# Adding up squares with accumulating transfers instead of VectorE, in a Strassen-like matmul with GELU

## The chip, the cores and the metric

The kernel runs on one core of a Trainium2 chip. Its time is the device time of one execution in microseconds; three executions gave 1578.17, 1579.82 and 1580.01 us, so the median before the change is 1579.82 us. The profile is of one more execution, with a span of 1577.1 us from the first to the last instruction and a granted TensorE clock of 0.999.

The engines are named as in the profile: PE is TensorE (PEld its weight loads), DVE is VectorE, ACT is ScalarE, POOL is GpSimd, and SP is SyncE. GpSimd issues all loads of this kernel, SyncE all stores.

## The reference

```python
def setup_inputs():
    m, k, n = 4096, 4096, 4096
    return {
        "a": np.random.randn(m, k).astype(np.float32),
        "b": np.random.randn(k, n).astype(np.float32),
    }

def reference(a, b):
    x = np.matmul(a, b)
    return 0.5 * x * (1 + np.tanh(np.sqrt(2 / np.pi) * (x + 0.044715 * x**3)))
```

The output is float32, 4096 x 4096.

## The kernel before

A and B are cast to float16 on their way in and cut into quadrants. Four quadrants of a block of the output (two times 512 rows by two times 512 columns) are made from seven products of sums of quadrants instead of eight plain products. That is one group; there are 16, numbered gi = 0 to 15. A group has 7 products s of 4 steps q each, 28 steps, and each step is 16 matmuls of 128x128 by 128x512. (Half of the first group is computed plainly, while its data come in: 16 plain steps and 14 others.) The products are accumulated in two chains of PSUM banks, X and Y, and between two products ScalarE or VectorE takes a copy of the banks:

```python
PRODUCTS = [
    ("M3", "Y", "11", ("12", "22", 1)),
    ("M5", "X", ("11", "12", -1), "22"),
    ("M7", "X", ("12", "22", -1), ("21", "22", 1)),
    ("M1", "X", ("11", "22", -1), ("11", "22", -1)),
    ("M4", "X", "22", ("21", "11", 1)),
    ("M2", "Y", ("22", "21", -1), "11"),
    ("M6", "Y", ("21", "11", -1), ("11", "12", 1)),
]
# ... cut
def multiply(gi, s, q):
    name, chain = product(gi, s)[:2]
    first = q == 0 and name in ("M3", "M5")
    sa, sb = sums.pop((gi, s, q))
    for i in range(RT):                       # RT = 4 banks
        acc = bank(gi, chain, i) if first else banks[chain, i]
        products(acc, sa, sb, i, first, q == QPH - 1)   # 4 matmuls, L331
        if q == QPH - 1:
            settle(gi, name, i)               # copies by ACT, sums by DVE, y
```

Such a copy is, for M5, `m5 = keep("m5", X, 2)`, a copy on ScalarE from PSUM (L395), after which VectorE makes `y = Y - m5`. M7, M1 and M4 go on in the same X banks.

VectorE makes the sums of quadrants that a step needs (L302), two steps ahead (AHEAD = 2), from A tiles (aT) and B tiles (bR) into aS and bS. The order of the program is the order on each engine; every engine works through its own queue in order:

```python
for n, step in enumerate(steps):
    for fn, args in before.get(n, ()):        # loads, transposes, squares, checks
        fn(*args)
    if n + AHEAD < len(steps):
        gi, s, q = steps[n + AHEAD]
        if s >= 0:
            make_sums(gi, s, q)
    if step[:2] != (0, 2):
        flush()
    combine()
    if step[1] < 0:
        plain(n)
    else:
        multiply(*step)
    if step == (0, 2, QPH - 1):
        flush()
```

Loads of the next group's B tiles stand in GpSimd's queue at steps 13, 15, 17 and 19 (8 transfers of 128 KB each) and at steps 25 and 27 (16 each).

The kernel also checks its inputs: it adds up the squares of all elements of A and B, by rows and columns, and takes another path (cut here) if they spread too far for float16. Half of the groups do this work: b in groups 1, 5, 9, 13 and a in groups 2, 6, 10, 14. A group has 32 pieces of 128x1024 elements, two a step for the first six steps and then one a step:

```python
def square(which, blk, quad, c, h):
    # ... src: a piece of an aT or bR tile
    half = quad[which == "b"]
    if half not in energy:
        t = energy[half] = pool.tile([P, W], BF16, name="energy", tag=f"energy{half}")
    else:
        t = pool.tile([P, W], BF16, name="square", tag="square", bufs=2)
        squares.append((half, t))
    nc.scalar.activation(t[:, :], src, ACT.Square)             # L207

def add_squares():
    for half, t in squares:
        tt(energy[half], energy[half], t, ALU.add)             # L431, on DVE
    squares.clear()

def weigh(which):          # DVE: an addition, a transpose and a reduction for each half
    ...

for mb in range(NMB):
    for which, gi in (("b", mb * NNB + 1), ("a", mb * NNB + 2)):
        # ... pieces: quadrants "22", "12", "21", "11"; c in 0, 1; h in 0..3
        n_two = len(pieces) - NP * QPH + 2
        for x, piece in enumerate(pieces):
            n = max(x // 2, x - n_two)
            at(gi, n // QPH, n % QPH, square, which, blk, *piece)
            at(gi, (n + 1) // QPH, (n + 1) % QPH, add_squares)
        at(gi, 6, 2, weigh, which)
```

So a group has two first squares, which go straight to `energy`, and 30 that go through the two buffers named `square` and are added.

Before the first data are there, TensorE multiplies zeros to keep its clock up:

```python
N_WARM = 46
def warm():
    z = pool.tile([P, NC], F16, name="zeros", tag="bS", bufs=AHEAD + 1)
    nc.vector.memset(z[:, :], 0.0)
    # ... banks
    for _ in range(N_WARM):
        nc.tensor.matmul(banks["X", RT - 1][:, :], z[:, :P], z[:, :], start=True, stop=True,
                         skip_group_check=True)                # L343
```

Of the kernel before, what the change touches and what calls it, by code (L numbers as in the profile page):

```python
# [13 lines left out]
ALU = mybir.AluOpType  # L14
# [10 lines left out]
AHEAD = 2  # L25
# [15 lines left out]
NP = len(PRODUCTS)  # L41
QPH = 4
# [6 lines left out]
    ("22", "21", "12", True), ("22", "22", "22", True),  # L49
]  # L50
N_PLAIN = 2 * len(PLAIN)
N_WARM = 46


SQUARE_MAX = 2.0**26
# [45 lines left out]
def half_path(  # L101
# [9 lines left out]
    nc = tc.nc  # L111
# [76 lines left out]
    def part(tiles, blk, quad, q):  # L188

        t = tiles[blk, quad, q // 2].rearrange("p x y -> p (x y)")  # L190
        w = 4 * NC
        return t[:, (q % 2) * w : (q % 2 + 1) * w]

    energy, squares = {}, []
# [13 lines left out]

    def add_squares():
        for half, t in squares:  # L210
            tt(energy[half], energy[half], t, ALU.add)
        squares.clear()

    def weigh(which):
# [63 lines left out]
    def product(gi, s):  # L278
        return (LAST if gi == len(groups) - 1 else PRODUCTS)[s]

    def make_sums(gi, s, q, only=None, h=None):

        mb, nb = groups[gi]
        _, _, oa, ob = product(gi, s)
        got = []
        for tiles, blk, o, tag in ((a_tiles, mb, oa, "aS"), (b_tiles, nb, ob, "bS")):
            if only not in (None, tag):
                continue
            if isinstance(o, str):
                got.append(part(tiles, blk, o, q))  # L290
                continue
            t = sums.pop((tag, gi, s, q), None)
            if t is None or h:
                if t is None:
                    t = pool.tile([P, 4 * NC], F16, name=tag, tag=tag, bufs=AHEAD + 1)
                x, y, z = t[:, :], part(tiles, blk, o[0], q), part(tiles, blk, o[1], q)
                if h is not None:
                    x, y, z = (
                        v.rearrange("p (jj m) -> p jj m", jj=2)[:, :, h * TM : (h + 1) * TM]
                        for v in (x, y, z)  # L300
                    )
                nc.vector.tensor_tensor(  # L302
                    out=x, in0=y, in1=z, op=ALU.add if o[2] > 0 else ALU.subtract
                )
            got.append(t)
            if tag == only:
                sums[tag, gi, s, q] = t
                return
        sums[gi, s, q] = got
# [10 lines left out]
    def bank(gi, chain, i):  # L320
        par = (gi + (chain == "Y")) % 2
        t = psum_pool.tile([P, NC], F32, name=f"acc{chain}", tag=f"bank{par}{i}")
        banks[chain, i] = t
        return t
# [11 lines left out]
# [3 lines that stand above are left out]
        for i in range(RT):  # L339
            bank(0, "X", i)  # L340
            bank(0, "Y", i)
        for _ in range(N_WARM):
            nc.tensor.matmul(  # L343
                banks["X", RT - 1][:, :], z[:, :P], z[:, :], start=True, stop=True, skip_group_check=True
            )

    def plain(n):

        (quad, oa, ob, by_rows), h = PLAIN[n // 2], n % 2
        chain = "X" if quad == "11" else "Y"  # L350
        seen = [x for x in range(len(PLAIN)) if PLAIN[x][0] == quad]
        sa, sb = a_tiles[0, oa, 0], b_tiles[0, ob, 0]
        sa = sa.rearrange("p jj (m e) -> p jj m e", e=2)
        tiles = [(j, e) for j in range(NJ // 2) for e in range(2) if by_rows or e == h]
        for i in range(h * RT // 2, (h + 1) * RT // 2) if by_rows else range(RT):
            acc = banks[chain, i]
            kept = quad in ("11", "22")
            start = (n // 2 == seen[0] or not kept) and (by_rows or h == 0)
            stop = (n // 2 == seen[-1] or not kept) and (by_rows or h == 1)
            c = f"c{quad}"  # L360
            for j, e in tiles:
                nc.tensor.matmul(
                    acc[:, :], sa[:, j, i * P : (i + 1) * P, e], sb[:, 2 * j + e, :],
                    start=start and (j, e) == tiles[0], stop=stop and (j, e) == tiles[-1],
                    skip_group_check=True,
                )
            if not stop:
                continue
            if not kept and n // 2 == seen[1]:
                tt(post[c, i], post[c, i], acc, ALU.add)  # L370
            elif quad == "12":
                post[c, i] = keep("x1", acc, RT)
            elif quad == "11":
                tt(post["c12", i], post["c12", i], acc, ALU.add)
            elif quad == "21":
                tag = ("energy1", "energy2", "square", "square")[i]
                t = pool.tile([P, W], BF16, name="c21", tag=tag, bufs=1 + (i > 1)).bitcast(F32)
                nc.scalar.copy(out=t[:, :], in_=acc[:, :])
                post[c, i] = t
            else:  # L380
                tt(post["c12", i], post["c12", i], acc, ALU.subtract)
# [5 lines that stand above are left out]
        for i in range(RT):  # L387
            acc = bank(gi, chain, i) if first else banks[chain, i]
            products(acc, sa, sb, i, first, q == QPH - 1)
            if q == QPH - 1:  # L390
                settle(gi, name, i)
# [8 lines left out]
    def flush():  # L400

        for args in waiting:
            gi, i, ih, jh, y, _ = args
            plain_part = post.pop((f"c{ih + 1}{jh + 1}", i), None) if gi == 0 else None
            if plain_part is not None:
                tt(y, y, plain_part, ALU.add)
            emit(*args)
        waiting.clear()
# [3 lines left out]
    def combine():  # L412

        for gi, i in later:
            x7, x1 = post["x7", i], post["x1", i]
            tt(x7, x1, x7, ALU.subtract)
            tt(x1, banks["Y", i], x1, ALU.subtract)
        later.clear()

    def emit(gi, i, ih, jh, y, src):  # L420
        mb, nb = groups[gi]
        nc.scalar.activation(y[:, :], src[:, :], ACT.Gelu_apprx_tanh)  # L422
        r0 = ih * MH + mb * TM + i * P
        c0 = jh * NH + nb * NC
        nc.sync.dma_start(out=out[r0 : r0 + P, c0 : c0 + NC], in_=y[:, :])
# [4 lines left out]
    def tt(o, x, y, op):  # L430
        nc.vector.tensor_tensor(out=o[:, :], in0=x[:, :], in1=y[:, :], op=op)  # L431
# [40 lines left out]
    steps = [(0, -1, n) for n in range(N_PLAIN)]  # L472
# [5 lines left out]
    def at(gi, s, q, fn, *args):  # L478
        if gi == 0 and s >= 0:
            q = max(q, QPH // 2)  # L480
        before.setdefault(position[gi, s, q], []).append((fn, args))


    for n, whats in (
# [10 lines left out]
        for what in whats.split():  # L495
            half = what[-1] == "0" and what != "A11_0" or what in ("A22_1", "T22_1")
# [52 lines left out]
    for mb in range(NMB):  # L549
        for which, gi in (("b", mb * NNB + 1), ("a", mb * NNB + 2)):  # L550
# [6 lines left out]
            for x, piece in enumerate(pieces):  # L557
                n = max(x // 2, x - n_two)
# [18 lines left out]
    at(len(groups) - 1, 2, 2, answer)  # L577
    at(len(groups) - 1, 4, 0, read)

    with tc.manual_schedule():  # L580
        warm()
        table = pool.tile([P, 1], F32, name="table", tag="table")
        nc.vector.memset(table[:, :], 0.0)
        nc.scalar.activation(table[:, :], table[:, :], ACT.Gelu_apprx_tanh)
        for n, step in enumerate(steps):
            for fn, args in before.get(n, ()):
                fn(*args)
            if n + AHEAD < len(steps):
                gi, s, q = steps[n + AHEAD]
                if s >= 0:  # L590
                    make_sums(gi, s, q)
            if step[:2] != (0, 2):
                flush()
            combine()
# [3 lines that stand above are left out]
                multiply(*step)  # L598
            if step == (0, 2, QPH - 1):
                flush()  # L600
        flush()
    return said["value"]


def kernel(tc: tile.TileContext, a: bass.AP, b: bass.AP, out: bass.AP):
    stands = half_path(tc, a, b, out)
    with tc.If(stands == 0):
        general_path(tc, a, b, out)
# [30 lines left out]
```

## Time and profile before

| what | value |
|---|---|
| time, median of 3 | 1579.82 us |
| span of the profile | 1577.1 us |
| TensorE busy | 1567.7 us, 7246 products |
| VectorE busy | 1233.7 us |
| ScalarE busy | 518.0 us |
| GpSimd busy (issuing transfers) | 537.7 us |
| DMA packets | 225047, 211.13 MB |
| HBM | 285.22 MB read, 67.11 MB written |

In a line of the groups stand the source line, the engine, the operation, what is written and read with its shape, how often, then the busy time in us and the mean of one in ns, and after the second bar the idle time of the engine just before these instructions and what ended most of it. A line of the waits names who waited for whom, the total in us, how often, and the longest. A line of the timeline begins with the start and the duration in us, and ends, in brackets, with the engine's idle time ahead of it and what ended that. For a transfer, the duration on POOL is the time to issue it; the time to landing is counted from the start of that issue to the semaphore that tells of its last byte.

### The profile page before, as it was taken

How to read it: one execution, taken by the hardware profiler on the slowest of the kernel's cores; microseconds unless marked ns; L12 is line 12 of the kernel's file. 1: busy time of each engine (PE TensorE's matmuls, PEld its weight loads, DVE VectorE, ACT ScalarE, POOL GpSimd, SP SyncE). 2: the span in 40 equal slices, each digit the busy share in tenths (PEclk: the TensorE clock that was granted, in tenths of full speed). 3: DMA queues.
4: the chain of work that ended last, by engine and by line, in shares of the span. 5: the costliest groups of instructions: out<-in, count | busy, mean ns of one | idle time of the engine just before them, and what ended most of it. 6: DMA issues, size and time to landing. Idle time of an engine off the chain costs nothing. (4 is left out here: it accounts for less than half of the span.)

```text
span 1577.1 us, 19678 instructions
## 1 busy us (share of the span) xinstructions
PE 1567.7 (99%) x7246; PEld 709.6 (45%) x7246; DVE 1233.7 (78%) x1381; ACT 518.0 (33%) x710; POOL 537.7 (34%) x980
## 2 busy tenths in 40 slices
PE   9999999999999999999999999999999999999998
PEld 4444444444444444444444444444444444444443
DVE  1698888967787888895778778887687778988775
ACT  1036445311122545531111344542211145364111
POOL 7753442420234144341124413245011443314400
PEclk9999999999999999999999999999999999999999
DMA  9999884882968378686597937679468885747802
GB/s 173 198 215 189 132 162 79 161 162 48 193 106 158 87 131 160 108 179 115 87 161 117 186 72 142 146 113 182 79 121 146 134 160 93 151 105 134 161 28 82
DMA packets 225047, 211.13 MB, mean 134 GB/s; under 512 B 20144, under 2 KB 192176, under 8 KB 224944
## 3 DMA queue, kind: packets, MB, share of 16 engines
q0 software_dynamic: 187648, 142.67, 61.7%
q1 hardware_dynamic: 37296, 67.13, 11.8%
q8 instruction: 59, 0.97, 0.2%
q14 instruction: 44, 0.36, 0.1%
HBM read 285.22 MB, written 67.11 MB: 223 GB/s over the span
## 5 line engine op out<-in xcount | busy, mean ns | idle before, releaser
L331 PEld LDWEIGHTS <-aS 128*128 128x128 f16 x4960 | 485.3, 98 | 587.2 <-issue 2.2
L186 POOL DMA_DIRECT2D bR<-in_b_dram x832 | 447.6, 544 | 700.0 <-DVE bS L302 329.7
L302 DVE TENSOR_TENSOR aS<-aT 128x2048 f16<-128x2048 f16 (+1 forms) x312 | 376.1, 1212 | 151.0 <-PE accX L331 114.5
L331 PE MATMUL accX<-bS,aS 128*128 128x512 f16 x1984 | 431.1, 379 | 0.0
L302 DVE TENSOR_TENSOR bS<-bR 128x2048 f16<-128x2048 f16 x310 | 376.1, 1218 | 69.3 <-PE accX L331 58.5
L331 PEld LDWEIGHTS <-aT 128*128 128x128 f16 x1984 | 194.2, 98 | 234.8 <-issue 0.8
L422 ACT ACTIVATE y<-y 128x512 f32<-128x512 f32 x192 | 118.5, 630 | 351.8 <-DVE y L431 351.4
L331 PE MATMUL accY<-bS,aS 128*128 128x512 f16 x992 | 216.7, 379 | 1.8 <-DVE y L431 1.8
L331 PE MATMUL accY<-bS,aT 128*128 128x512 f16 x992 | 216.9, 379 | 0.5 <-DVE bS L302 0.5
L331 PE MATMUL accX<-bS,aT 128*128 128x512 f16 x992 | 216.7, 379 | 0.0
L331 PE MATMUL accX<-bR,aS 128*128 128x512 f16 x992 | 216.7, 379 | 0.0
L331 PE MATMUL accY<-bR,aS 128*128 128x512 f16 x992 | 216.7, 379 | 0.0
L186 POOL DMA_DIRECT2D stage<-in_a_dram x144 | 89.9, 630 | 249.0 <-DVE aT L161 178.0
L431 DVE TENSOR_TENSOR energy<-energy,square 128x1024 bf16<-128x1024 bf16 x240 | 164.4, 685 | 9.5 <-ACT square L207 5.7
L395 ACT COPY x<-accX 128x512 f32<-128x512 f32 x128 | 74.9, 585 | 224.3 <-PE accX L331 224.3
L207 ACT ACTIVATE square<-aT 128x1024 bf16<-128x1024 f16 x120 | 123.4, 1051 | 70.6 <-DVE energy L431 70.2
L207 ACT ACTIVATE square<-bR 128x1024 bf16<-128x1024 f16 x120 | 123.0, 1050 | 62.5 <-DVE energy L431 60.5
L161 DVE STREAM_TRANSPOSE aT<-stage 128x2048 uint32<-128x2048 uint32 (+1 forms) x37 | 74.6, 2017 | 46.0 <-DMA stage<-in_a_dram 39.9
L395 ACT COPY m<-accX 128x512 f32<-128x512 f32 x60 | 34.7, 579 | 215.7 <-PE accX L331 213.6
L422 ACT ACTIVATE y<-accX 128x512 f32<-128x512 f32 x64 | 38.2, 597 | 100.1 <-PE accX L331 99.9
L431 DVE TENSOR_TENSOR x<-accX,x 128x512 f32<-128x512 f32 x64 | 44.0, 691 | 21.8 <-ACT y L422 19.1
L431 DVE TENSOR_TENSOR y<-accY,m 128x512 f32<-128x512 f32 x60 | 39.9, 687 | 12.5 <-ACT m L395 12.4
(38 smaller groups left out, 344.9 us busy)
## 6 DMA issues: line engine op xcount, KB each, us to landing
bR<-in_b_dram POOLq DMA_DIRECT2D x832, 128.0 KB, 5.2
out_dram<-y SPq DMA_DIRECT2D x256, 256.0 KB, 5.7
stage<-in_a_dram POOLq DMA_DIRECT2D x112, 256.0 KB, 6.8
stage<-in_a_dram POOLq DMA_DIRECT2D x32, 128.0 KB, 5.1
row<-seen_d SPq DMA_DIRECT2D x2, 1.5 KB, 4.2
seen_d<-seen SPq DMA_DIRECT2D x1, 3.0 KB, 7.4
```

The source lines that it names most:

```text
L161: nc.vector.transpose(dst[:, :, x, :], src[:, :, x, :])
L186: nc.gpsimd.dma_start(out=dst, in_=src)
L207: nc.scalar.activation(t[:, :], src, ACT.Square)
L302: nc.vector.tensor_tensor(out=x, in0=y, in1=z, op=ALU.add if o[2] > 0 else ALU.subtract)
L331: nc.tensor.matmul(acc[:, :], sa[:, j // 2, i * P : (i + 1) * P, j % 2], sb[:, j, :], start=start and j == 0, stop=stop and j == 3, skip_g ...
L395: nc.scalar.copy(out=t[:, :], in_=src[:, :])
L422: nc.scalar.activation(y[:, :], src[:, :], ACT.Gelu_apprx_tanh)
L431: nc.vector.tensor_tensor(out=o[:, :], in0=x[:, :], in1=y[:, :], op=op)
```

## The change

Three things change. The squares are no longer added by VectorE (`tt`) but by transfers from GpSimd's queue that add what they read to what stands at their destination, both in on-chip memory: 128 partitions x 1024 bf16 elements, 256 KB, 30 for each of the eight groups. This is to take 240 instructions off VectorE. Second, in the first group the sums for M6's last step are made after the step that ends M2, so that VectorE comes to M2's y first and TensorE gets M6's banks earlier. (The sums concerned are named `late`.) Third, there are 39 warm products instead of 46.

```diff
-N_WARM = 46
+N_WARM = 39
...
     def add_squares():
         for half, t in squares:
-            tt(energy[half], energy[half], t, ALU.add)
+            nc.gpsimd.dma_start(out=energy[half][:, :], in_=t[:, :], accum_op=ALU.add)
         squares.clear()
...
+    late = (0, NP - 1, QPH - 1)
+
     with tc.manual_schedule():
...
             if n + AHEAD < len(steps):
-                gi, s, q = steps[n + AHEAD]
-                if s >= 0:
-                    make_sums(gi, s, q)
+                ahead = steps[n + AHEAD]
+                if ahead[1] >= 0 and ahead != late:
+                    make_sums(*ahead)
             if step[:2] != (0, 2):
                 flush()
...
             if step == (0, 2, QPH - 1):
                 flush()
+            if step == (0, NP - 2, QPH - 1):
+                make_sums(*late)
         flush()
```

In the order of the changed kernel's instructions each of these transfers waits for the one before it into the same half, for ScalarE's square, and for the transfer that last used its semaphore; a square waits for the transfer that read its buffer two squares ago. In GpSimd's queue a group's 30 additions stand as 16, a burst of 8 loads, 2, 8 loads, 2, 8 loads, 2, 8 loads, 6, 16 loads, 2, 16 loads.

## The prediction

> **What bounds the kernel now.** I read the page first (shares of the engines, then the groups), then who waited for whom, then the timeline of the first 45 us and of the stretch from 215 to 315 us, which is one of the groups that the squares belong to, and last the time to landing of each kind of transfer. The chain of waits on the page holds a single link (ACT, 0%) and says nothing here.
>
> ```profile
> PE 1567.7 (99%) x7246; PEld 709.6 (45%) x7246; DVE 1233.7 (78%) x1381; ACT 518.0 (33%) x710; POOL 537.7 (34%) x980
> ```
>
> TensorE is busy 99% of the span. The timeline shows 32 products starting at 14.37 and the next 32 at 21.27, so one step of 16 products takes 3.45 us. 7246 less 46 warm ones are 7200 products, 450 steps, 1553 us. Together with the 14.4 us ahead of them and about 6 us behind the last product's start this is 1573 of 1577.1 us: TensorE waits for about 4 us in all. No part of the change can win more than that, since it removes no product that counts.
>
> ```profile
> L431 DVE TENSOR_TENSOR energy<-energy,square 128x1024 bf16<-128x1024 bf16 x240 | 164.4, 685 | 9.5 <-ACT square L207 5.7
> L207 ACT ACTIVATE square<-aT 128x1024 bf16<-128x1024 f16 x120 | 123.4, 1051 | 70.6 <-DVE energy L431 70.2
> L207 ACT ACTIVATE square<-bR 128x1024 bf16<-128x1024 f16 x120 | 123.0, 1050 | 62.5 <-DVE energy L431 60.5
> ```
>
> These groups are what the change touches: 240 additions of 685 ns on VectorE. The reader is to see the last column: ScalarE's squares already wait 130.7 us for VectorE's additions to free one of the two square buffers. That idle time costs nothing today, but it is the hook on which a slower adder pulls. Who pulls next is seen in the waits:
>
> ```profile
> ACT m L395 <- PE accX L331: 213.6, 30, 45.8
> ACT square L207 <- DVE energy L431: 130.7, 96, 4.7
> ...
> PE accY L331 <- DVE y L431: 1.8, 1, 1.8
> ```
>
> The last line is one of the few waits of TensorE: 1.8 us, once. In the timeline it stands at 113.72, the start of M6 in the first group: VectorE makes M6's last operand sums (110.72 and 111.85) ahead of y (112.99), and M6 needs the bank that y empties.
>
> ```profile
> 220.45 1.04 ACT L207 ACTIVATE energy<-aT 128x1024 bf16<-128x1024 f16 x1
> ...
> 237.34 2.00 ACT L207 ACTIVATE square<-aT 128x1024 bf16<-128x1024 f16 x2 [3.75 <-DVE energy L431]
> 243.25 0.58 ACT L395 COPY m<-accX 128x512 f32<-128x512 f32 x1 [3.90 <-PE accX L331]
> ```
>
> ```profile
> 141.05 1.76 POOL L186 DMA_DIRECT2D bR<-in_b_dram  x3 [0.20 <-issue]
> 163.05 4.27 POOL L186 DMA_DIRECT2D bR<-in_b_dram  x8 [20.25 <-DVE energy L431]
> ```
>
> ```profile
> 229.17 0.54 POOL L186 DMA_DIRECT2D bR<-in_b_dram  x1 [0.80 <-DMA bR<-in_b_dram]
> 260.25 4.28 POOL L186 DMA_DIRECT2D bR<-in_b_dram  x8 [30.54 <-DVE bS L302]
> ```
>
> The first of these is ScalarE in group 2, which starts at 218.0: fourteen squares stand in its in-order queue ahead of the m copies, which empty M5's banks. Today they are through by 239.3 and ScalarE then waits 3.9 us for TensorE. The two others are GpSimd's queue: the loads that stand in front of the squares' additions are issued until 142 us in group 1 (start 120.6) and until 229.7 in group 2.
>
> ```profile
> L186 POOL DMA_DIRECT2D bR<-in_b_dram x832: 542/542/579, 4.2 to 1486.5; - x167
> ...
> DMA to landing us min/median/max: 2.8/5.2/9.7
> ```
>
> ```profile
> q0 software_dynamic: 187648, 142.67, 61.7%
> q1 hardware_dynamic: 37296, 67.13, 11.8%
> ```
>
> A 128 KB load issued by GpSimd takes 2.8 us at the least from issue to landing. The two queues give the time of a packet: 0.617 x 16 x 1577.1 / 187648 = 83 ns on q0, 0.118 x 16 x 1577.1 / 37296 = 80 ns for the 2 KB rows of the stores on q1.
>
> **What the Trainium skill says.** "DMA: Bandwidth & Descriptors", Anatomy of one DMA (SWDGE path), gives some 2.0 us fixed for such a transfer, mostly completion, plus its bytes. The trace agrees: 2.8 us less 128 packets / 16 engines x 83 ns = 0.66 leaves 2.1. The same page, Rules for kernel authors, says that nothing holds the bytes between an accumulate's read and its write, and that the next must wait for the earlier one's semaphore; in the order of the changed kernel every addition waits for the one before it. "Collectives: The Full Stack", the bandwidth ceiling in Part 3, says that an add in the DMA engine costs two source reads and so runs at half the rate of a copy; no run here shows that yet. "TensorE: Matmul & The Clock Gate", Part 1, says that after an idle window of about 3.4 us the array restarts at half clock; here the first warm products start 0.43 us apart and later ones 0.216, so it can be seen at the start at least.
>
> **The change part by part.**
> 1. 39 warm products. The 46 end at about 14.1 us (the first 13 at 0.43 us, the other 33 at 0.2157: 1.42 + 5.6 + 7.1), and the transpose that releases the first real product ends at 11.75 + 2.37 = 14.12. Both end together, so seven fewer give at best 0.2 us; the 1.5 us of idle time that they leave is short of an idle window. I count 0.
> 2. The sums moved behind y. y can follow the sums at 109.58, and M6 starts where M2 ends. The moved sums then end near the start of M6's last step and may give 0.4 us back. I count 1.5 us won.
> 3. VectorE loses 240 x 0.685 = 164 us. TensorE hardly waits for it (one 0.5 us wait for bS in group 1), so I count 0.5 us.
> 4. The squares, in 8 of the 16 groups (1, 2, 5, 6, 9, 10, 13, 14), 30 additions each. They become one serial chain on GpSimd's queue: each needs the landing of the one before. Its period p is the 2.8 us, less 0.66, plus an estimate of 128 x 2 KB rows read twice, 8 x 2 x 80 ns = 1.28, which gives 3.4; with 0.2 us to pick up the semaphore (the gap between POOL issues in the timeline) p = 3.6 us. The chain then stops TensorE in three places of a group.
>
> **M5's copies.** In a b group (1, 5, 9, 13) thirteen buffered squares stand ahead of the copies, with two buffers, so the copies need the 11th addition, one more square (1.05) and a copy (0.6). In an a group a second first square needs no buffer, and it is the 10th. Group 1: the last load ahead is issued at 142.3, the first addition lands behind the queued loads at about 148.6, ten more make 184.6, the copy is done at 186.3; M7 needs the bank at 120.6 + 8 x 3.45 = 148.2. Stall 38 us. Groups 5, 9, 13: the loads ahead end 10.7 us after the group's start, not 22, so 27 us. The a groups follow a stalled group, their loads ahead end some 8.5 us after the start, and they need nine more: 21 us. 38 + 3 x 27 + 4 x 21 = 203.
>
> **M1's and M4's copies** (steps 15 and 19). Between them stand four additions, 14.4 us, against four steps, 13.8, and a burst of 8 loads of B for each two additions. A burst takes 8 x 0.66 = 5.3 us of the DMA engines, of which I add 4 us to the chain. By step 15 the chain is 1 us late in a b group and 4.5 in an a group; by step 19 two bursts add 14.4 + 8 - 13.8 = 8.6. About 10 and 13 us: 4 x 10 + 4 x 13 = 92.
>
> **The weighing at step 26.** VectorE must wait for the last addition, and the next group's first sum is behind it. Eight additions, a burst of 8 and one of 16 (10 us): 28.8 + 14 = 42.8, less the 1.7 by which the copies trail; then weighing 4.15 us (308.77 to 312.92 in the timeline of VectorE) and a sum of 1.2, against 8 steps, 27.6. Stall 19, and 8 x 19 = 152.
>
> Sum: 1579.8 - 2 + 203 + 92 + 152 = 2025. A transfer that reads SBUF should land somewhat earlier than the HBM load that I took p from, so I choose 2000.
>
> **The rivals.**
> (a) The chain is hidden: additions land fast enough for ScalarE and the loads. For it: VectorE's slack grows and POOL is busy for only 34%. Against it: 11 additions in the 16 us that group 2 leaves between 229.7 and 245.6 need 1.4 us each, half of the fastest landing in the profile. Time 1577.
> (b) Only throughput counts: 240 x 128 packets x 160 ns / 16 = 307 us more on engines that are some 74% busy. In the groups of the squares (70 to 82% busy in the view by stretches) 38 us are added to 97, about 10 to 20 us over: 1580 + 8 x 15 = 1700.
> (c) The adder in the DMA engine is slow, far below half rate: p of 6 us instead of 3.6 adds 30 x 2.4 x 8 = 576 us: about 2600.
> (d) The clock: each stall over a window restarts TensorE with 13 products at half clock, 2.8 us. Up to 24 stalls make 67 us, but what follows is bound by the chain again, so most of it vanishes in the next stall. I add nothing.
>
> **Range and chances.** The time moves by 240 us for each microsecond of p, since the chain has 240 links. p from 2.6 to 4.9 gives about 1760 to 2320, and I hold that at 8 in 10. Faster by over 2% would be more than the 4 us there are: 0.01. Within 2% needs rival (a): 0.05. Slower: 0.94.
>
> **What would show it.** Right: GpSimd's additions follow each other at 3 to 4.5 us; ScalarE's squares wait for those transfers; TensorE waits for ScalarE (copies of m) at the start of M7 in eight groups, 20 to 40 us each, and for VectorE's sums at the start of the next group behind a wait of the weighing; groups 0, 3, 4, 7, 8, 11, 12, 15 keep their 96.7 us; no wait of M6 in the first group. Wrong: landings of 2 us or less with TensorE still at 99%; DMA engines near full with additions landing late because of bytes, not of their order; or long waits of TensorE for B tiles, which I do not expect, because the loads of the next group stand 15 steps ahead of their use.

## The result and the profile after

The changed kernel takes 2127.28 us (median, 2120.36 to 2133.84) against 1579.28 for the kernel before: the ratio is 1.347, 95% interval 1.344 to 1.350. The profiled execution spans 2118.8 us, 541.7 more than before, with a mean granted TensorE clock of 0.888.

The shares of the engines, from the page of the changed kernel:

```profile
PE 1626.0 (77%) x7239; PEld 721.2 (34%) x7239; DVE 1086.6 (51%) x1141; ACT 516.4 (24%) x710; POOL 753.2 (36%) x1220
```

VectorE is relieved as intended, by 147 us. TensorE now stands idle for 23% of a longer span, and no engine is near full: this is a kernel bound by latency. The groups that tell so:

```profile
L331 PE MATMUL accX<-bS,aS 128*128 128x512 f16 x1984 | 445.8, 387 | 194.9 <-ACT m L395 193.6
...
L211 POOL DMA_DIRECT2D energy<-square x240 | 211.6, 882 | 728.6 <-DMA energy<-square 383.4
...
L331 PE MATMUL accY<-bS,aT 128*128 128x512 f16 x992 | 233.2, 399 | 208.1 <-DVE bS L302 208.1
...
L207 ACT ACTIVATE square<-bR 128x1024 bf16<-128x1024 f16 x120 | 126.3, 1055 | 389.0 <-DMA energy<-square 388.9
```

After the second bar the first of these two groups of matmuls, which stood idle for 0.0 and 0.5 us in the kernel before, waits 194.9 us, 193.6 of them for ScalarE's copies of M5, and the second 208.1 us for VectorE's first sum of a group. ScalarE's squares wait for the transfers, and GpSimd, which issues the transfers, waits for the transfers. The same ring in the waits:

```profile
ACT square L207 <- DMA energy<-square: 732.0, 204, 19.6
...
PE accY L331 <- DVE bS L302: 208.1, 9, 27.8
DVE square L220 <- DMA energy<-square: 199.6, 7, 30.3
PE accX L331 <- ACT m L395: 193.6, 9, 38.1
...
PE accY L331 <- DVE aS L302: 54.1, 8, 9.3
```

The counts are the reader's clue: eight groups add squares, and TensorE's long waits come in eights and nines, not spread over the 112 products. How long a landing takes, from the view of the transfers' destination:

```profile
L211 POOL DMA_DIRECT2D energy<-square x240: 860/869/998, 143.9 to 2004.8; - x120
...
DMA to landing us min/median/max: 3.2/3.3/9.0
```

Now the ring link by link, in group 1. GpSimd's timeline, then ScalarE's, then TensorE's:

```profile
180.28 0.87 POOL L211 DMA_DIRECT2D energy<-square  x1 [2.95 <-DMA energy<-square]
184.07 0.87 POOL L211 DMA_DIRECT2D energy<-square  x1 [2.92 <-DMA energy<-square]
187.88 0.87 POOL L211 DMA_DIRECT2D energy<-square  x1 [2.94 <-DMA energy<-square]
```

```profile
183.62 1.06 ACT L207 ACTIVATE square<-bR 128x1024 bf16<-128x1024 f16 x1 [2.73 <-DMA energy<-square]
187.43 1.06 ACT L207 ACTIVATE square<-bR 128x1024 bf16<-128x1024 f16 x1 [2.76 <-DMA energy<-square]
188.40 1.05 ACT L395 COPY m<-accX 128x512 f32<-128x512 f32 x2
```

```profile
136.91 13.98 PE L331 MATMUL accX<-bR,aS 128*128 128x512 f16 x64
189.02 26.34 PE L331 MATMUL accX<-bS,aS 128*128 128x512 f16 x112 [38.13 <-ACT m L395]
```

The addition issued at 184.07 is the group's eleventh. It lands at 187.4, the thirteenth square starts at 187.43, the copy of M5's first bank ends at 189.0, and M7 starts at 189.02, 38.1 us late. The end of the group, GpSimd's timeline first, then VectorE's and TensorE's:

```profile
271.35 0.87 POOL L211 DMA_DIRECT2D energy<-square  x1 [2.96 <-issue]
271.91 4.67 POOL L186 DMA_DIRECT2D bR<-in_b_dram  x8
...
284.27 0.96 POOL L211 DMA_DIRECT2D energy<-square  x1
290.11 0.87 POOL L211 DMA_DIRECT2D energy<-square  x1 [4.89 <-issue]
```

```profile
293.69 0.42 DVE L220 TENSOR_TENSOR square<-energy 128x512 bf16<-128x512 bf16 x1 [28.57 <-DMA energy<-square]
...
297.30 2.35 DVE L302 TENSOR_TENSOR bS<-bR 128x2048 f16<-128x2048 f16 x2
```

```profile
298.57 15.82 PE L331 MATMUL accY<-bS,aT 128*128 128x512 f16 x64 [25.50 <-DVE bS L302]
```

VectorE stands for 28.6 us in front of the weighing, with the next group's sums behind it in its queue. By stretches, groups 1 to 4 (the columns are span, then busy time and instructions of PE, PEld, DVE, ACT, POOL, then granted clock, DMA share, GB/s):

```profile
118.80:298.60 179.80, 103.46 (x450) 45.16 (x449) 65.56 (x72) 48.67 (x62) 74.41 (x119) 0.80 0.76 136
298.60:455.20 156.60, 105.97 (x449) 45.81 (x449) 65.82 (x71) 47.55 (x60) 61.39 (x95) 0.83 0.73 132
455.20:553.90 98.70, 98.70 (x448) 44.26 (x448) 72.70 (x71) 16.81 (x29) 17.01 (x27) 0.98 0.61 109
553.90:650.60 96.70, 96.70 (x449) 43.84 (x448) 71.57 (x70) 17.11 (x30) 32.52 (x60) 1.00 0.79 137
```

Groups 1 and 2 lose 83 and 60 us against the 96.7 us of before. Group 3 takes 98.7 us, its first products at a lower rate after the stop ahead of it, and group 4 takes 96.7. The DMA engines are busy for 0.76 and 0.73 of the time in groups 1 and 2 and for 0.79 in group 4, which loses nothing.

Summed over the starts of all products of the trace, the loss splits into idle time of TensorE at step 8 of the groups (194 us), at steps 16 and 22 (28 and 55), at step 0 of the next group (207), and some 55 us in which it ran at less than full rate after such a stop: 539 of the 541.7 us.

### The profile page after: what moved, and what is told of

Its sections match the earlier page's. It is cut to its first block, busy times and chain, and to the rows that moved or that the text cites. A ratio compares the mean times of both kernels' runs of the same rounds, so it can differ in the third digit from the quotient of the medians.

```text
span 2118.8 us, 19959 instructions
## 1 busy us (share of the span) xinstructions
PE 1626.0 (77%) x7239; PEld 721.2 (34%) x7239; DVE 1086.6 (51%) x1141; ACT 516.4 (24%) x710; POOL 753.2 (36%) x1220
## 5 line engine op out<-in xcount | busy, mean ns | idle before, releaser
L331 PEld LDWEIGHTS <-aS 128*128 128x128 f16 x4960 | 492.2, 99 | 861.6 <-issue 238.9
L331 PE MATMUL accX<-bS,aS 128*128 128x512 f16 x1984 | 445.8, 387 | 194.9 <-ACT m L395 193.6
L186 POOL DMA_DIRECT2D bR<-in_b_dram x832 | 464.5, 675 | 254.4 <-PE accX L331 87.3
L211 POOL DMA_DIRECT2D energy<-square x240 | 211.6, 882 | 728.6 <-DMA energy<-square 383.4
L331 PE MATMUL accY<-bS,aT 128*128 128x512 f16 x992 | 233.2, 399 | 208.1 <-DVE bS L302 208.1
L331 PEld LDWEIGHTS <-aT 128*128 128x128 f16 x1984 | 199.9, 101 | 490.2 <-issue 272.1
L331 PE MATMUL accY<-bR,aS 128*128 128x512 f16 x992 | 234.5, 399 | 54.1 <-DVE aS L302 54.1
L331 PE MATMUL accX<-bS,aT 128*128 128x512 f16 x992 | 224.7, 389 | 26.7 <-ACT x L395 26.7
L220 DVE TENSOR_TENSOR square<-energy 128x512 bf16<-128x512 bf16 x16 | 8.9, 553 | 227.9 <-DMA energy<-square 199.6
```

The source lines that it names most:

```text
L186: nc.gpsimd.dma_start(out=dst, in_=src)
L211: nc.gpsimd.dma_start(out=energy[half][:, :], in_=t[:, :], accum_op=ALU.add)
L220: nc.vector.tensor_tensor(out=u[:, :NC], in0=pair[:, 0, :], in1=pair[:, 1, :], op=ALU.add)
L331: nc.tensor.matmul(acc[:, :], sa[:, j // 2, i * P : (i + 1) * P, j % 2], sb[:, j, :], start=start and j == 0, stop=stop and j == 3, skip_g ...
```

## The experiments

The theory: each addition waits for the landing of the one before, and three in-order queues carry that delay to TensorE. The main rival: the bytes of the additions load the DMA engines. Others: too few buffers, late B tiles, and loss from the two small parts.

### The small parts alone

VectorE adds the squares again; the sums stay moved, 39 warm products stay.

```diff
-            nc.gpsimd.dma_start(out=energy[half][:, :], in_=t[:, :], accum_op=ALU.add)
+            tt(energy[half], energy[half], t, ALU.add)
```

> The two small parts alone: the sums moved behind y in the first group and 39 warm products, while VectorE adds the squares as before. If the accumulating transfers carry the whole loss, this is not slower than before: 1577 to 1579 us, 1.5 us won at M6 in the first group and 0 to 1.2 us at the first real product (13.15 us in the changed kernel's profile, 14.37 before). If the small parts carry some of the loss, it is above 1590 us.

Measured: 1580.76 us against 1579.13, ratio 1.0010 (1.0003 to 1.0017). The transfers carry the whole loss. But the small parts do not win the 1.5 us that were expected of them here; they lose 1.6. So each was run alone.

> Only the sums moved behind y, 46 warm products: the 1.9 us gap ahead of M6 in the first group goes, and at most 0.5 us comes back at M6's last step: 1577.5 to 1578.5 us. If the moved sums come too late for the last step, no gain: 1579.5.

Measured: 1580.52, ratio 1.0005 (0.9997 to 1.0014).

> Only 39 warm products. If the first transpose ends at 14.1 us in most executions, no gain: 1579.3 us. If the data usually come earlier and the 46 warm products held the first real one back, up to 1.2 us won: 1578.1. A longer idle time that drops the clock would cost about 2.8 us: 1582.

Measured: 1579.52, ratio 1.0003 (0.9995 to 1.0012). The first real product starts at 13.6 us in this profile, 14.37 before, so something was won there; nothing of it reached the end.

Why the moved sums win nothing is in TensorE's timeline. Before:

```profile
113.72 7.07 PE L331 MATMUL accY<-bS,aS 128*128 128x512 f16 x32 [1.77 <-DVE y L431]
120.62 7.07 PE L331 MATMUL accY<-bS,aT 128*128 128x512 f16 x32
128.23 5.12 PE L331 MATMUL accY<-bS,aT 128*128 128x512 f16 x23 [0.54 <-DVE bS L302]
```

With only the sums moved:

```profile
113.07 7.35 PE L331 MATMUL accY<-bS,aS 128*128 128x512 f16 x32
120.25 7.07 PE L331 MATMUL accY<-bS,aT 128*128 128x512 f16 x32
130.54 2.72 PE L331 MATMUL accY<-bS,aT 128*128 128x512 f16 x6 [3.22 <-DVE bS L302]
```

The gap ahead of M6 is gone, and a longer one stands four steps further on, ahead of step 2 of group 1. VectorE's timeline of the same kernel names its source:

```profile
117.80 2.49 DVE L431 TENSOR_TENSOR y<-y,c 128x512 f32<-128x512 f32 x4
...
125.94 0.69 DVE L431 TENSOR_TENSOR y<-accY,x 128x512 f32<-128x512 f32 x1 [3.91 <-DMA out_dram<-y]
```

The moved sums now stand ahead of `y + c21` (116.51 before, 117.80 here), so the stores of y leave 1.3 us later; there are five y tiles, and the second y of M6 waits for such a store to land. That store also takes 6.6 us to land instead of 5.4, for which no run gives a reason. The stores set the time, not the order of the sums; the version with two more y tiles, below, tests this. Here the stop costs more than its length: the 8 products after it start some 0.4 us apart instead of 0.216, 1.5 us more. The granted clock was 0.998 or less in 14 of the 34 executions of this kernel and of the small parts together, and in none of 41 of the kernel before the change.

### A copy instead of an addition

```diff
-            nc.gpsimd.dma_start(out=energy[half][:, :], in_=t[:, :], accum_op=ALU.add)
+            nc.gpsimd.dma_start(out=energy[half][:, :], in_=t[:, :])
-RATIO = 4.0
+RATIO = 2.0**20
```

The kernel leaves out the additions; its check is of single squares.

> The same 240 transfers in the same order and with the same waits, but they copy and do not add (the sums of squares are then wrong, and the bound on their spread is raised so that the main path is taken). If two reads per row are what makes an adding packet take 187 ns, a copy's packet takes 80 to 100 ns, the landing falls from 3.3 to about 2.5 us, the period from 3.8 to 3.0, and the time to about 2127 - 240 x 0.8 = 1935 us. If the latency is all fixed (issue, completion), the landing stays at 3.2 to 3.3 and the time at 2100 or more. If the adding itself stalled the engines, the landing falls below 2.3.

Measured: 1961.5 us, one execution. The view of the transfers' destination:

```profile
DMA to landing us min/median/max: 2.2/2.3/9.1
```

The landing falls by 1.0 us, and the additions' period from 3.82 to 2.82. In the packet records the copy moves 4096 bytes in 171 ns, the addition 2048 bytes in 187: from the start of a transfer's first packet to the end of its last it is 0.8 us for the copy and 1.5 for the addition, 0.7 of the 1.0. The other 0.3 lie ahead of the first packet: the issue is shorter too, 0.55 us against 0.87. So an addition costs twice the copy's time per byte, and still most of the 3.3 us is there without any addition. The time falls by 166 us, less than 240 x 1.0: by the starts of the products the stalls at step 8 fall by 80 us, those at steps 16 and 22 by 33, and those at step 0 by 39.

### Two chains, more buffers

The pieces of the two halves take turns:

```diff
-                (quad, c, h) for quad in ("22", "12", "21", "11")
-                for c in range(CH) for h in range(NJ // 2)
+                (quad, c, h)
+                for pair in ((("22", "21"), ("12", "11")) if which == "b" else (("22", "12"), ("21", "11")))
+                for c in range(CH) for h in range(NJ // 2) for quad in pair
```

> The pieces of the two halves take turns, so that each addition waits for the landing of the one before the last instead of the last one; bytes, transfers and buffers are unchanged. If the serial chain is the cause, two additions are in flight, a pair takes 3.3 landing + 0.2 + 1.05 square + 0.5 pickup = 5.1 us, 2.6 us each instead of 3.8: the stalls at step 8 fall by some 12 us each, those at 16 and 22 go, those of the weighing fall by 10: about 1810 us. If the bytes of the DMA engines are the cause, nothing changes: 2127.

Measured: 1811.44 us, ratio 1.148 (1.146 to 1.150). The same bytes in the same number of transfers, and 316 us less: the rival of the bytes falls. By the starts of the products the stalls at step 8 fall from 194 to 71 us, those at steps 16 and 22 go, and those at step 0 fall from 207 to 123. In the b groups the new order also puts the second first square, which needs no buffer, ahead of step 8, so one addition fewer stands there; by an estimate from the period that is at most 4 x 3.8 = 15 of the 316 us. GpSimd's timeline of this kernel:

```profile
155.16 0.87 POOL L211 DMA_DIRECT2D energy<-square  x1 [2.59 <-DMA energy<-square]
156.67 0.87 POOL L211 DMA_DIRECT2D energy<-square  x1 [0.64 <-ACT square L207]
159.90 0.87 POOL L211 DMA_DIRECT2D energy<-square  x1 [2.36 <-DMA energy<-square]
161.45 0.87 POOL L211 DMA_DIRECT2D energy<-square  x1 [0.69 <-ACT square L207]
```

Two additions go out each 4.74 us, and half of them now wait for the square, which waits for a buffer.

Three buffers for squares, with one fewer for y, on the single chain:

```diff
-            t = pool.tile([P, W], BF16, name="square", tag="square", bufs=2)
+            t = pool.tile([P, W], BF16, name="square", tag="square", bufs=3)
...
-        return pool.tile([P, NC], F32, name="y", tag="y", bufs=5)
+        return pool.tile([P, NC], F32, name="y", tag="y", bufs=4)
```

(The other tiles that stand in the same buffers get three as well.)

> Three buffers for squares instead of two (one fewer for y, to make room), the chain as it was. If the chain is the cause, the additions still follow each other at 3.8 us and ScalarE is ahead by one square more: the copies at step 8 need one addition fewer, 8 x 3.8 = 30 us less there, given back in part at the weighing, which needs all of them: 2095 to 2127. If it were the buffers that hold things up, the period would fall and with it the time, below 2000.

Measured: 2119.09, ratio 1.342 (1.339 to 1.344), so 8 us less than the changed kernel. By the starts of the products the stalls at step 8 fall from 194 to 158 us and those at step 0 rise from 207 to 237: the buffer moved the wait and did not shorten the chain.

> Both: two chains and three buffers. If the chain is the cause, squares are ready in time and a pair of additions takes 3.3 + 0.5 = 3.8 us, 1.9 each: left are the stalls at step 8 in the b groups (about 19 and 3 x 11 us) and some 11 us at each weighing: about 1720 us. If bytes bound it, 2127.

Measured: 1761.73, ratio 1.117 (1.114 to 1.119). Now the same buffer is worth 50 us, since squares had become the limit; the additions follow each other at 1.9 us, as expected. The time is 40 us above what I expected: the stalls at step 0 are 13.3 to 16.1 us and not 11, which is 28 us more in all, and I had left out 29 us lost at less than full rate. The stalls at step 8 came out 17 us shorter, 35 us in all and not 52.

### The weighing later

```diff
-        at(gi, 6, 2, weigh, which)
+            if which == "a" and mb < NMB - 1:
+                at(gi + 1, 2, 0, weigh, which)
+            else:
+                at(gi, 6, 2, weigh, which)
```

> VectorE weighs the squares of A in groups 2, 6 and 10 ten steps later, at step 8 of the group after (where no squares are made). If the in-order queue of VectorE, blocked by the weighing's wait for the last addition, is what stops TensorE for 25.4, 25.8 and 26.3 us at the start of groups 3, 7 and 11, these three stalls go: 2127 - 78 = about 2050 us. If late loads of B tiles stop TensorE there, they stay: 2127.

Measured: 2046.68, ratio 1.297 (1.295 to 1.299), 81 us less. The three stalls are gone from the starts of groups 3, 7 and 11 (2.1 us at step 10 came in their place); TensorE runs through the start of group 3:

```profile
425.90 13.98 PE L331 MATMUL accY<-bS,aT 128*128 128x512 f16 x64
439.72 13.98 PE L331 MATMUL accX<-bR,aS 128*128 128x512 f16 x64
```

No bracket, so no wait; and the loads of B stand where they stood. It was VectorE's queue behind the weighing, not late tiles.

All three steps together:

> Two chains, three buffers, and the weighing of A in groups 2, 6 and 10 moved to step 8 of the group after. The stalls at the start of groups 3, 7 and 11 (14.4, 14.5 and 15.2 us with two chains and three buffers) go with what their restart costs: 1761 - 44 - 6 = about 1712 us. If this gain is not additive to the others, above 1740.

Measured: 1715.22, ratio 1.086 (1.085 to 1.088). The three stalls go, as expected, for 47 us; on the single chain, where they were longer, the same step had won 81. With all three steps adding by transfers stays 136 us slower than adding on VectorE.

### Only the squares of B by transfers

```diff
...
+            if which_now[0] == "b":
                 nc.gpsimd.dma_start(out=energy[half][:, :], in_=t[:, :], accum_op=ALU.add)
+            else:
+                tt(energy[half], energy[half], t, ALU.add)
```

> Only the squares of B are added by transfers, those of A by VectorE as before. If each group's chain stops TensorE by itself, the four b groups lose what they lost in the changed kernel, and the groups after them the stall at their start: from its profile 129 us at step 8, 10 at step 16, 33 at step 22, 102 at the start of the next group and some 25 at half clock, together about 300: 1880 us. If the a groups had suffered only because b groups made them late, more of the loss stays: above 1950.

(`which_now` holds which matrix the squares come from.) Measured: 1876.19, ratio 1.188 (1.186 to 1.190). Each group's chain stops TensorE by itself.

### A version that beats both

The small parts failed for want of y tiles. In the first group the tiles of m are free by then:

```diff
-    def new_y():
+    def new_y(spare=False):
+        if spare:
+            return pool.tile([P, NC], F32, name="y", tag="m5", bufs=2)
         return pool.tile([P, NC], F32, name="y", tag="y", bufs=5)
...
         elif name == "M6":
-            y = new_y()
+            y = new_y(gi == 0 and i < 2)
```

> The two small parts on the kernel before (VectorE adds the squares), and in the first group two of M6's four y tiles stand in the buffers of m, which are free then, so that VectorE does not wait for stores of y to land. The small parts alone won nothing, because the moved sums pushed the stores of C21 back and the fifth y waited for one to land: the gap of 1.9 us ahead of M6 came back as 3.5 instead of 0.7 us at the second step's sums of group 1. If that is so, the wait at group 1 goes and the gain stays: 1576 us, ratio 0.997 to 0.999. If VectorE is late there for another reason, as small_parts: 1580.5.

Measured: 1576.36 us against 1579.12, ratio 0.9982 (0.9976 to 0.9989): faster than both kernels, if by 2.8 us only. VectorE's timeline of this kernel:

```profile
119.42 1.88 DVE L433 TENSOR_TENSOR y<-accY,x 128x512 f32<-128x512 f32 x3
123.61 0.69 DVE L433 TENSOR_TENSOR y<-accY,x 128x512 f32<-128x512 f32 x1 [2.31 <-DMA out_dram<-y]
124.22 1.22 DVE L302 TENSOR_TENSOR bS<-bR 128x2048 f16<-128x2048 f16 x1
```

Three y come at once, only the fourth waits for a store, and the sum that came at 126.96 before is made at 124.22. No gap of over 0.6 us between products is left in the whole trace.

> Only the two y tiles in m's buffers, 46 warm products and the sums where they were. The wait of 0.7 us at group 1 goes, the gap of 1.9 us ahead of M6 stays: 1578.5 us, within the noise of before. If this alone gives as much as spare_y, the moved sums and the warm products are worth nothing at all.

Measured: 1578.13, ratio 0.9993 (0.9985 to 1.0002). The tiles alone are within the noise. The tiles, the moved sums and the warm products together give 1.8 us more than the tiles alone, with intervals that overlap slightly; what the small parts are worth shows only once the wait behind them is gone.

## Why the prediction was right or wrong

**The mechanism was right.** The chain, the three places where it stops TensorE, the groups that keep their time: all are in the profile where the prediction put them, one of the stops by another path. Both rivals that meant a small loss fell: the landing is not hidden, and bytes are not the cause (two_chains). A slow adder fell as well: 187 ns for 2 KB is 2.2 times the copy's 85.5, near the estimate of 160, and near the half rate that the Trainium skill gives ("Collectives: The Full Stack", the bandwidth ceiling in Part 3).

**The period was a little too short.** Landing 3.3 us (3.4 expected) plus 0.5 from a landing to the next issue, where I took 0.2 from gaps between issues that had nothing to wait for: p is 3.82 and not 3.6. That the landing came so near is partly luck: the packets take 1.5 us where I had 1.28, and the rest of it 1.8 where I had 2.1. So the part besides the packets was shorter than in the loads from HBM, as I had argued when I chose less than the sum, but packets and pickup took that back. The 240 us for each microsecond of p were too steep as well: the plain copy, 1.0 us less a link, won 166 us. In my own terms only 11 (in an a group 10), 4 and 8 links of a group stand ahead of a stop, 180 in all.

**M5's copies:** 203 us expected, 194 measured. Groups 5, 9 and 13 were expected at 27 and stood for 30, the a groups at 21 and stood for 16 to 17, so the sum is near because two errors cancel. Group 1 was expected at 38 and stood for 38.1, by luck: the copy is done at 189.0 and not 186.3, and TensorE is ready for it at 150.9 and not 148.2, both 2.7 us later than I had them.

**M1's and M4's copies:** 92 expected, 83 measured at steps 16 and 22. The second does not stop TensorE through the banks, as I thought, but through VectorE. Its timeline in group 1:

```profile
246.22 2.48 DVE L431 TENSOR_TENSOR x<-accX,x 128x512 f32<-128x512 f32 x4 [16.38 <-ACT y L422]
248.62 3.48 DVE L302 TENSOR_TENSOR aS<-aT 128x2048 f16<-128x2048 f16 x3
```

VectorE waits behind ScalarE's late y of M4, with the sums for M2 behind it.

**The weighing was the term that was mis-sized:** 152 us expected, 207 measured, some 26 each and not 19. In group 1 the addition of square 23 (counted from 0) is issued at 241.19 and that of square 31, the last, at 290.11; of the 6 us that this is longer than I had it, 8 x 0.22 = 1.8 are the period, 3.3 the burst of 8 loads at step 19 (241.19 to 256.09 in GpSimd's timeline: two periods of chain and burst take 14.9 us, 7.3 over 2 x 3.82, where I had 4), and 1.1 the burst of 16 (271.35 to 290.11: 18.8, so 11.1 over, where I had 10). Over all four bursts of 8 in that group the mean is 6.0 us.

**The clock:** I added nothing for it, and TensorE lost some 55 us at a lower rate after its stops: 64 products in 15.82 us after the stop at 298.57 instead of 13.98. Whether part of it was hidden, as I argued, was not tried; that group 2's stall at step 8 came out at 16 us instead of 21, in spite of the longer period, speaks for it. Against the 447 us that I had for the three places, stalls and slow running are 539. The profiled execution took 2120.4 us, 95 more than the sum of 2025: M5's copies -9, M1's and M4's -9, the weighing +55, the clock +55 and the small parts +2 make 94.

**The small parts were wrong:** 2 us won were expected (1.5 from the moved sums, 0.5 from VectorE's relief) and nothing came. The warm products were counted at 0 and gave 0 in the time, though the first real product did start earlier. The step that failed is "M6 starts where M2 ends ... I count 1.5 us won": the start came, and the stores of y took it back at step 2 of group 1 (counted from 0).

**The choice of 2000** instead of the sum of 2025 went the wrong way; the time lies inside the range because the range allowed for p up to 4.9. The measured p of 3.82 gives 2053 by the prediction's formula; most of the rest came from the bursts at the weighing and from the clock.

## What to carry to other kernels

Where each piece of work needs the one before, moving it from a busy engine to one with idle time is judged by the latency of a link, not by its busy time: here the accumulating transfers into one tile, each waiting for the one before, are a serial chain, 3.8 us a link against 0.685 us on VectorE, and every in-order queue that holds a link passes the delay on to what stands behind it. Before such a move, find what the producer waits for today (here ScalarE's squares already waited for the adder, at no cost) and work out these waits again with the new latency. And when a gap is closed and the time stays, look further down the timeline: the next limit (here the fifth y tile and the landing of a store) takes the gain until it is removed as well.

## What the hardware showed that was not expected

- An accumulating transfer of 128 x 2 KB moved in 2048-byte packets of 187 ns and took 0.87 us to issue; the plain copy between the same tiles moved in 4096-byte packets of 171 ns and took 0.55 us. Why the copy moves two rows in a packet and the addition one, no run shows.
- From the landing of a transfer to the start of the next issue that waited for it GpSimd needs 0.5 us, with additions and with copies alike.
- The length of a stop alone did not decide whether TensorE ran slower after it. At step 2 of group 1 stops of 2.5 us (the changed kernel) and 3.2 us (only the sums moved) left the 8 products after them some 0.4 us apart, so that 32 products of the changed kernel took 8.66 us instead of 7.07; stops of 2.9 us (the weighing later) and 3.4 us (the small parts) left none slower. The Trainium skill ("TensorE: Matmul & The Clock Gate", Part 1) says that the window of the clock gate runs free of what the kernel does. The traces agree: in their records of the granted clock every stretch between the first and the last is a multiple of 3.41 us. I cut the 14 traces into these windows and counted each product as 0.216 us of work. After a window at full clock with an idle share of 0.637 or more the clock was halved, 164 times of 164; with 0.636 or less it never was. The stop of 2.5 us fell into one window (0.74 idle, with the pause between two products), that of 3.4 us was split over two (0.63 and 0.40).
